# Two-layer diffusion block: all modulation vectors in the first layer, and later places for the block sums of a seven-product feed-forward

## The chip, the cores and the metric

The kernel runs on one core of one Trainium2 chip. The metric is the device time of one execution in microseconds (us); the time of a kernel is the median of its runs. The traces below are each of one profiled execution.

## The reference, cut to what matters

Two layers (`DEPTH = 2`) work on 256 image tokens `x` and 256 context tokens `ctx`, each of width 1024. A layer is a feed-forward, a token mixer (neighbourhood attention beside a pooling branch) and a second feed-forward, each between two norms and each modulated:

```
for l in range(DEPTH):
    mx = mod_vectors(c, w_mod[l], b_mod[l])          # silu(c) @ w_mod + b_mod, split in 9 vectors of 1024
    mc = mod_vectors(c_ctx, w_mod[l], b_mod[l])
    x   = x   + 0.5 * mx[2] * rms(swiglu(rms(x)   * (1 + mx[1]) + mx[0]))     # first feed-forward
    ctx = ctx + 0.5 * mc[2] * rms(swiglu(rms(ctx) * (1 + mc[1]) + mc[0]))
    x, ctx = token mixer with vectors 3, 4, 5
    x, ctx = second feed-forward with vectors 6, 7, 8 (ctx only where l is not the last)
```

A modulation vector depends on `c` and `c_ctx` and on nothing that the layers compute, so it may be computed at any time before it is used. In the last layer the context needs no vector from the sixth (number 5) on. The feed-forward has 2816 hidden columns, 22 blocks of 128. All matmuls are float32 made from two float32r parts, "hi" and "lo" (three matmuls for each product).

## The kernel before, in words

**Stages.** The program runs `ffn(0, 0)`, `token_mix(0)`, `ffn(0, 1)`, `ffn(1, 0)`, `token_mix(1)`, `ffn(1, 1)`. In the trace `ffn(0, 1)` takes from about 605 to 980 us, and `ffn(1, 0)` from about 980 to 1345 us.

**A feed-forward** works through groups of the 22 column blocks. For each block PE multiplies the input `h_big` with the gate and up weights (`pg_ps`, `pu_ps`); ACT and DVE make silu(gate) * up (`tt_wk`) and split it in hi and lo (`g_big`). After a group the down matmuls (`pd_ps`) go over its blocks. Every weight comes by a DMA on SP's queue into one of two `raw` buffers, is rounded to its hi part by ACT, and DVE subtracts to get the lo part (`w_big<-raw_raw,w_big`). All DMAs are issued by SP, in order.

**The seven-product feed-forward.** `ffn(1, 0)` alone (`SEVEN`) multiplies the gate and up weights with seven products of half blocks in the place of eight. After `LEAD = 3` ordinary blocks, each block needs four sums of weight parts on POOL (`prep_seven`: `s12`, `s34`, in the trace `s_wk<-raw_raw` and its like), two more splits on ACT and DVE, and a chain of additions on DVE of what the products leave in PSUM (`c_wk`, `u_wk`) ahead of `tt_wk` and `g_big`. The input needs sums too: `add_up` makes them on POOL in place (`yg_wk<-yg_wk`), and ACT and DVE split them (`ht_big`). The groups (`S_GROUPS`) are of 4, 4, 4, 4 and 6 blocks.

**The modulation.** The vectors 0 and 1 of layer 0 are computed by matmuls at the start. The other 16 lie in the list `todo`, nine steps each. Each of the first eight steps (`mod_steps`) loads 512 KB of `w_mod` (`wm_wk`) and accumulates it on DVE (`acc_wk<-wm_wk,csil`), once for each of the two token streams, or once only for the vectors 5 to 8 of the last layer. The ninth moves each accumulator to another layout with eight 64 KB DMAs (`part_wk<-acc_wk`), folds it with three additions on POOL, sums over partitions with a small matmul (`pm_ps<-sel,part_wk`) and finishes on DVE (`col`); for the vectors 2, 5 and 8 a transposition (`pr_ps`) and one more DMA follow. `fill(rate)`, called after each block of a feed-forward, takes `rate` further steps from the list; `RATE` is 2.6 in the first three feed-forwards.

**The order.** Nothing is issued when it is written. The functions record operations (`Recorder.record`), and `Recorder.order` makes one list out of them: it goes through the operations with prices of its own, and takes next, on the engine that is free first, the one that can start earliest, and among such the one recorded first. An operation's `margin` puts off the time at which this planner thinks it ready. Buffers are places that the planner gives out as well. So the order on each engine is fixed when the program is built, and each engine runs its own list in order, whatever the real times are: an instruction that waits holds up all that stand behind it on its engine.

Of the kernel before, what the change touches and what calls it, by code (L numbers as in the profile page):

```python
# [35 lines left out]
LEAD = 3  # L36
# [3 lines left out]
LIMITS = {"ps": 1}  # L40
RATE = 2.6
BEHIND = 0
MARGIN = 6.0
# [356 lines left out]
def tile_dit_block(  # L400
# [56 lines left out]
    class Stream:  # L457
        def __init__(self):
            self.plan = []
            self.ready = []  # L460
            self.raws = []
            self.taken = 0
            self.ahead = AHEAD

        def add(self, src, parts, seven=False):
# [284 lines left out]
    class Input:  # L750
# [21 lines left out]
        def add_up(self):  # L772
# [3 lines left out]
            for o in range(2):  # L776
                one, two = self.full[ORDER[o]], self.full[ORDER[2 + o]]
                a, b, c, d = one[:, lower, :], two[:, lower, :], two[:, upper, :], one[:, upper, :]
                nc.gpsimd.tensor_sub(a, b, a)
                nc.gpsimd.tensor_sub(b, c, b)  # L780
                nc.gpsimd.tensor_sub(c, c, a)
                nc.gpsimd.tensor_sub(d, d, c)
                for i, src in enumerate((a, c, b, d)):
                    dst = self.sums[i][:, :, :, o * P : (o + 1) * P]
                    split(dst[:, 0], dst[:, 1], src)
# [136 lines left out]
    def ffn(l, ff, both, nxt, rate, lead, parts):  # L922
# [27 lines left out]
        def gate_up(fs, parts):  # L950
# [3 lines left out]
            for part in parts:  # L954
                for f, wg, wup, pg, pu in held:
                    if seven:
# [5 lines left out]
                    if part is parts[-1]:  # L962
                        gate_up_evac(f, pg, pu)
                if seven and part is parts[0]:
                    H["now"].add_up()

# [45 lines left out]
        for gi, (f0, f1) in enumerate(groups):  # L1012
# [4 lines left out]
            elif gi == 0:  # L1017
                gate_up(tuple(range(lead)), parts)
                f = lead
                fill(lead * rate)  # L1020
            while f < f1:
# [4 lines left out]
                f += 1  # L1026
                fill(rate)
            if gi + 1 < len(groups):
# [346 lines left out]
    token_mix(0, (0, 6))  # L1375
    ffn(0, 1, True, (1, 0), RATE, LEAD, (CS, XS))
    ffn(1, 0, True, (1, 3), RATE, LEAD, (0, 1))
    token_mix(1, (1, 6))
    ffn(1, 1, False, None, 0.0, 0, None)

# [105 lines left out]
```

## Time and profile before

| | |
|---|---|
| median of 3 runs | 1677.81 us (1677.76 to 1678.05) |
| the profiled execution | 1681.01 us, its span from the first to the last instruction 1679.1 us |
| mean granted TensorE clock | 0.990 |
| PE busy | 1624.4 us (97%), 9074 matmuls |
| DVE busy | 1276.3 us (76%) |
| ACT, POOL busy | 729.0 us (43%), 363.7 us (22%) |
| DMA | 269.11 MB, mean 160 GB/s |

Idle time of an engine that does not bound the time costs nothing. The page's busy time for PE counts matmuls as pipelined, with ends that are modelled; a gap in it is a time in which PE had nothing it could run. In the timeline a row is: start in us, length in us, engine, line, operation, out<-in, count, and in brackets the engine's idle time before it with what ended it. In a table of stages ("windows") the columns are the stretch, its length, then for each engine its busy time and the count of its instructions, the granted TensorE clock, the DMA engines' share and GB/s. In a list of groups, the busy time and the mean ns of one stand behind the first bar, the idle time before and its releasers behind the second.

### The profile page before, as it was taken

The numbers are of one execution on the slowest core, as the hardware profiler recorded it, in microseconds if no ns is written. First come the engines' busy times: TensorE is split into PE (matmuls) and PEld (weight loads), VectorE is DVE, ScalarE is ACT, GpSimd is POOL, SyncE is SP. The second block draws the span as 40 slices with busy tenths as digits, with TensorE's granted clock in tenths as the row PEclk, the third lists the DMA queues.
The fourth block names the chain that finished last, engine by engine and source line by source line (L and its number), as shares of the span: only waits on it lengthen the run. The fifth ranks groups of instructions, "written<-read, shape, count | busy, mean of one in ns | idle before, by whom it ended". The sixth has DMA issues, their size and how long they took to land.

```text
span 1679.1 us, 23648 instructions
## 1 busy us (share of the span) xinstructions
PE 1624.4 (97%) x9074; PEld 1396.6 (83%) x9074; DVE 1276.3 (76%) x1748; ACT 729.0 (43%) x1287; POOL 363.7 (22%) x348
## 2 busy tenths in 40 slices
PE   6999999999999999999999988999999999899998
PEld 4988888888877798888888888979889888779997
DVE  7987876556789689967745499899989788975664
ACT  7422322225566562232222273433434567664442
POOL 1011111102133211120110064362754022210000
PEclk9999999999999999999999999999999999999999
DMA  9467656631222425765554216354323412355551
GB/s 377 165 233 245 226 176 217 200 104 66 89 73 86 158 101 206 249 212 202 197 187 164 100 42 230 132 187 168 121 101 105 163 57 100 123 199 191 201 197 57
DMA packets 98960, 269.11 MB, mean 160 GB/s; under 512 B 9424, under 2 KB 39328, under 8 KB 87072
## 3 DMA queue, kind: packets, MB, share of 16 engines
q1 hardware_dynamic: 98848, 267.60, 45.7%
q8 instruction: 72, 1.18, 0.3%
q14 instruction: 40, 0.33, 0.1%
HBM read 251.80 MB, written 1.09 MB: 151 GB/s over the span
## 4 chain that ended last, share of the span: by engine, by line
PE 74%; DVE 12%; ACT 5%; issue 3%; DMA 2%; POOL 2%; SPq 1%; POOLq 0%; DVEq 0%; ACTq 0%
PE pd_ps L382 22%; PE pg_ps L382 19%; PE pu_ps L382 19%; PE p_ps L382 6%; DVE w_big L382 3%; PE pk_ps L382 2%; PE pv_ps L382 2%; ACT n_wk L382 2%; POOL rs_st L382 2%; PE pq_ps L382 1%; DVE acc_wk L382 1%; DMA w_big<-in_wmod_dram 1%; ACT sx_wk L382 1%; DVE tt_wk L382 1%; PE pt_ps L382 1%
## 5 line engine op out<-in xcount | busy, mean ns | idle before, releaser
L382 DVE TENSOR_TENSOR w_big<-raw_raw,w_big 128x1024 fp32r<-128x1024 f32 x293 | 374.5, 1291 | 103.2 <-ACT w_big L382 102.5
L382 PE MATMUL pd_ps<-w_big,g_big 128*128 128x512 f32 x1848 | 437.6, 397 | 9.9 <-ACT g_big L382 7.0
L382 PEld LDWEIGHTS pd_ps<-w_big,g_big 128*128 128x128 f32 x1848 | 347.9, 189 | 91.5 <-ACT g_big L382 7.9
L382 ACT ACTIVATE w_big<-raw_raw 128x1024 fp32r<-128x1024 f32 x293 | 302.6, 1053 | 230.9 <-DMA raw_raw<-in_wgu_dram 92.2
L382 PE MATMUL pu_ps<-h_big,w_big 128*128 128x512 f32 (+1 forms) x1944 | 367.8, 342 | 0.0
L382 PEld LDWEIGHTS pu_ps<-h_big,w_big 128*128 128x128 f32 x1944 | 305.6, 189 | 42.6
L382 PE MATMUL pg_ps<-h_big,w_big 128*128 128x512 f32 (+1 forms) x1752 | 331.0, 343 | 2.6 <-ACT h_big L382 1.7
L382 PEld LDWEIGHTS pg_ps<-h_big,w_big 128*128 128x128 f32 x1752 | 276.0, 189 | 43.6 <-ACT h_big L382 2.6
L382 DVE SCALAR_TENSOR_TENSOR acc_wk<-wm_wk,csil,acc_wk 128x1024 f32<-128x1024 f32 x196 | 249.5, 1307 | 41.4 <-DMA wm_wk<-in_wmod_dram 41.3
L382 POOL TENSOR_TENSOR part_wk<-part_wk 128x512 f32<-128x512 f32 (+2 forms) x84 | 89.5, 1066 | 474.6 <-DMA part_wk<-acc_wk 380.8
L382 ACT ACTIVATE g_big<-tt_wk 128x512 fp32r<-128x512 f32 (+1 forms) x84 | 49.2, 585 | 285.5 <-DVE tt_wk L382 283.5
L382 POOL TENSOR_SCALAR rs_st<-sq_st 128x1 f32<-128x1 f32 x24 | 8.3, 346 | 521.0 <-ACT n_wk L382 520.9
L382 POOL TENSOR_TENSOR s_wk<-raw_raw 128x512 f32<-128x512 f32 x38 | 67.4, 1784 | 92.3 <-DMA raw_raw<-in_wgu_dram 39.9
L382 PE MATMUL p_ps<-h_big,w_big 128*128 128x256 f32 x684 | 86.7, 280 | 0.0
L382 PE MATMUL p_ps<-ht_big,w_big 128*128 128x256 f32 x684 | 84.1, 281 | 0.0
L382 PEld LDWEIGHTS p_ps<-h_big,w_big 128*128 128x128 f32 x684 | 83.5, 189 | 0.3
L382 PEld LDWEIGHTS p_ps<-ht_big,w_big 128*128 128x128 f32 x684 | 82.2, 189 | 0.0
L382 ACT ACTIVATE tt_wk<-pg_ps 128x512 f32<-128x512 f32 (+1 forms) x67 | 35.9, 536 | 96.2 <-PE pg_ps L382 73.9
L382 DVE TENSOR_TENSOR g_big<-tt_wk,g_big 128x512 fp32r<-128x512 f32 (+1 forms) x84 | 59.4, 707 | 21.3 <-ACT g_big L382 21.1
L382 DVE TENSOR_TENSOR y_big<-y_big,pd_ps 128x512 f32<-128x512 f32 x72 | 47.1, 680 | 36.0 <-PE pd_ps L382 36.0
L382 PE MATMUL pd_ps<-w_big,mix_big 128*128 128x512 f32 x288 | 72.0, 399 | 0.5 <-DVE mix_big L382 0.5
L382 DVE SCALAR_TENSOR_TENSOR tt_wk<-tt_wk,pg_ps 128x512 f32<-128x512 f32 (+1 forms) x67 | 41.0, 612 | 34.1 <-ACT tt_wk L382 33.6
(159 smaller groups left out, 1851.0 us busy)
## 6 DMA issues: line engine op xcount, KB each, us to landing
raw_raw<-in_wgu_dram SPq DMA_DIRECT2D x84, 1024.0 KB, 4.9
wm_wk<-in_wmod_dram SPq DMA_DIRECT2D x128, 512.0 KB, 6.2
raw_raw<-in_wdn_dram SPq DMA_DIRECT2D x44, 1024.0 KB, 5.1
part_wk<-acc_wk SPq DMA_DIRECT2D x224, 64.0 KB, 2.5
raw_raw<-in_wkq_dram SPq DMA_DIRECT2D x8, 1024.0 KB, 4.7
raw_raw<-in_wout_dram SPq DMA_DIRECT2D x8, 1024.0 KB, 4.9
w_big<-in_wmod_dram SPq DMA_DIRECT2D x7, 1024.0 KB, 12.6
gb_wk<-grow SPq DMA_DIRECT2D x10, 512.0 KB, 6.0
```

Of the source, the lines that this page charges most:

```text
L382: getattr(getattr(nc, op.engine), op.method)(*[self.real(a) for a in op.args], **{k: self.real(a) for k, a in op.kw.items()})
```

## The change

Three things are changed. First, `rate` becomes one number for each group of a feed-forward: 2.6 throughout in `ffn(0, 0)` as before, then 2.6, 4.2 and 5.6 in the three groups of `ffn(0, 1)`, and 0 in `ffn(1, 0)`. With 8, 8 and 6 blocks that is 57 steps and then 88, where 144 are to be done; before it was 57, 57 and the remaining 30. Second, `add_up` is recorded in the middle of the second half of the input in place of the end of the first half, with a margin for the first of its subtractions. Third, the first weight sum of the first seven-product block gets a margin of 12 us in the planner's time.

```diff
-RATE = 2.6
+RATE = (2.6, 2.6, 2.6)
+LATER = (2.6, 4.2, 5.6)
+NONE = (0.0,) * 5
...
+            rec.margin = 0.0 if self.sevens else 2 * MARGIN
+            self.sevens += 1
             nc.gpsimd.tensor_add(s12[:, 0, :], a21, a22)
+            rec.margin = 0.0
...
+                rec.margin = MARGIN
                 a, b, c, d = one[:, lower, :], two[:, lower, :], two[:, upper, :], one[:, upper, :]
                 nc.gpsimd.tensor_sub(a, b, a)
+                rec.margin = 0.0
...
-                for f, wg, wup, pg, pu in held:
+                for i, (f, wg, wup, pg, pu) in enumerate(held):
+                    if seven and part is parts[1] and i == 1:
+                        H["now"].add_up()
...
-                if seven and part is parts[0]:
-                    H["now"].add_up()
...
-                fill(lead * rate)
+                fill(lead * rate[gi])
...
-                fill(rate)
+                fill(rate[gi])
...
-    ffn(0, 1, True, (1, 0), RATE, LEAD, (CS, XS))
-    ffn(1, 0, True, (1, 3), RATE, LEAD, (0, 1))
+    ffn(0, 1, True, (1, 0), LATER, LEAD, (CS, XS))
+    ffn(1, 0, True, (1, 3), NONE, LEAD, (0, 1))
     token_mix(1, (1, 6))
-    ffn(1, 1, False, None, 0.0, 0, None)
+    ffn(1, 1, False, None, NONE, 0, None)
```

Where the instructions move, at three places. PE's own list keeps its order but for the small matmuls of the modulation (`pm_ps`, `pr_ps`).

DVE, the end of the first seven-product block (the fourth of its group) in `ffn(1, 0)`. `c_wk` and `u_wk` gather the products, `tt_wk` is silu(gate) * up, `g_big` its lo part; `w_big` and `wb_wk` are splits of weights of later blocks. Before:

```order
985 L382 TENSOR_TENSOR u_wk_8344<-p_ps_8367,c_wk_8383 128x512
986 L382 TENSOR_TENSOR col_100<-col_100,colt 128x8
987 L382 TENSOR_TENSOR w_big_8300<-raw_raw_8097,w_big_8300 128x1024
988 L382 TENSOR_TENSOR c_wk_8383<-p_ps_8367,u_wk_8344 128x256
989 L382 TENSOR_TENSOR w_big_8319<-raw_raw_8097,w_big_8319 128x1024
990 L382 TENSOR_TENSOR c_wk_8383<-p_ps_8400,u_wk_8344 128x512
991 L382 TENSOR_TENSOR w_big_8430<-raw_raw_8371,w_big_8430 128x1024
992 L382 SCALAR_TENSOR_TENSOR tt_wk_8455<-tt_wk_8455,c_wk_8383 128x512
993 L382 TENSOR_TENSOR wb_wk_8441<-raw_raw_8371,wb_wk_8441 128x512
994 L382 TENSOR_TENSOR tt_wk_8455<-tt_wk_8455,c_wk_8383 128x512
995 L382 TENSOR_TENSOR g_big_8336<-tt_wk_8455,g_big_8336 128x512
```

And the changed kernel at the same place:

```order
1010 L384 TENSOR_TENSOR wb_wk_8487<-raw_raw_8423,wb_wk_8487 128x512
1011 L384 TENSOR_TENSOR u_wk_8461<-p_ps_8491,c_wk_8494 128x512
1012 L384 TENSOR_TENSOR c_wk_8494<-p_ps_8491,u_wk_8461 128x256
1013 L384 TENSOR_TENSOR wb_wk_8529<-raw_raw_8469,wb_wk_8529 128x512
1014 L384 TENSOR_TENSOR w_big_8541<-raw_raw_8423,w_big_8541 128x1024
1015 L384 TENSOR_TENSOR c_wk_8494<-p_ps_8522,u_wk_8461 128x512
1016 L384 SCALAR_TENSOR_TENSOR tt_wk_8572<-tt_wk_8572,c_wk_8494 128x512
1017 L384 TENSOR_TENSOR tt_wk_8572<-tt_wk_8572,c_wk_8494 128x512
1018 L384 TENSOR_TENSOR g_big_8453<-tt_wk_8572,g_big_8453 128x512
```

Nine accumulations (`acc_wk`) that stood between the head of this feed-forward and this point (rows 961 to 983) are gone, two splits from `raw_raw_8097` that stood between `u_wk` and `c_wk` come earlier (rows 1005 and 1007, `raw_raw_8238`), and no split stands between the last `c_wk` and `g_big`.

POOL, the head of `ffn(1, 0)`: the norms of its input (`rs_st`) and the four weight sums of the first seven-product block (`s_wk`). Before:

```order
165 L382 TENSOR_TENSOR rs_st_7758<-rs_st_7758,nhalf 128x1
166 L382 TENSOR_TENSOR s_wk_7798<-raw_raw_7631 128x512
167 L382 TENSOR_TENSOR s_wk_7798<-s_wk_7798,raw_raw_7631 128x512
168 L382 TENSOR_TENSOR s_wk_7803<-raw_raw_7631 128x512
169 L382 TENSOR_SCALAR rs_st_7812<-sq_st_7767 128x1
170 L382 TENSOR_TENSOR rs_st_7812<-rs_st_7812,nhalf 128x1
171 L382 TENSOR_TENSOR s_wk_7803<-raw_raw_7631,s_wk_7798 128x512
```

And the changed kernel:

```order
177 L384 TENSOR_TENSOR rs_st_7910<-rs_st_7910,nhalf 128x1
178 L384 TENSOR_TENSOR s_wk_7946<-raw_raw_7789 128x512
179 L384 TENSOR_SCALAR rs_st_7957<-sq_st_7919 128x1
180 L384 TENSOR_TENSOR rs_st_7957<-rs_st_7957,nhalf 128x1
181 L384 TENSOR_TENSOR s_wk_7946<-s_wk_7946,raw_raw_7789 128x512
182 L384 TENSOR_TENSOR s_wk_7983<-raw_raw_7789 128x512
183 L384 TENSOR_TENSOR s_wk_7983<-raw_raw_7789,s_wk_7946 128x512
```

The first sum stays where it was, and the next two now stand behind one more norm. The sums of the input (`yg_wk<-yg_wk`) stood behind the last of the eight norms before and stand there now.

DVE, the down matmuls of the second group of `ffn(0, 1)` (`y_big` adds what they leave). Before, three accumulations in this stretch:

```order
844 L382 TENSOR_TENSOR w_big_6907<-raw_raw_6814,w_big_6907 128x1024
845 L382 TENSOR_TENSOR w_big_6947<-raw_raw_6814,w_big_6947 128x1024
846 L382 TENSOR_TENSOR w_big_6987<-raw_raw_6899,w_big_6987 128x1024
847 L382 TENSOR_TENSOR y_big_6074<-y_big_6074,pd_ps_6865 128x512
848 L382 TENSOR_SCALAR acc_wk_7011<-wm_wk_6974,csil 128x1024
849 L382 TENSOR_TENSOR y_big_6074<-y_big_6074,pd_ps_6872 128x512
```

And the changed kernel, with twenty in it:

```order
856 L384 TENSOR_SCALAR acc_wk_6995<-wm_wk_6932,csil 128x1024
857 L384 SCALAR_TENSOR_TENSOR acc_wk_6995<-wm_wk_6953,csil,acc_wk_6995 128x1024
858 L384 TENSOR_TENSOR w_big_7010<-raw_raw_6879,w_big_7010 128x1024
859 L384 SCALAR_TENSOR_TENSOR acc_wk_6995<-wm_wk_6964,csil,acc_wk_6995 128x1024
860 L384 SCALAR_TENSOR_TENSOR acc_wk_6995<-wm_wk_6973,csil,acc_wk_6995 128x1024
861 L384 TENSOR_TENSOR w_big_7043<-raw_raw_6956,w_big_7043 128x1024
862 L384 SCALAR_TENSOR_TENSOR acc_wk_6995<-wm_wk_6987,csil,acc_wk_6995 128x1024
863 L384 TENSOR_TENSOR y_big_6076<-y_big_6076,pd_ps_6923 128x512
```

Each accumulation waits for its own DMA (`wm_wk`), and the splits and additions behind it wait with it.

More of the change, by code (lines that the diff above doesn't have):

```diff
@@ L463, in __init__ @@
             self.ahead = AHEAD
+            self.sevens = 0
         def add(self, src, parts, seven=False):
```

## The prediction

> **What bounds the kernel now.** I read the page first, then a table by stage, then the groups and the timeline where that table shows a loss.
>
> ```profile
> PE 1624.4 (97%) x9074; PEld 1396.6 (83%) x9074; DVE 1276.3 (76%) x1748; ACT 729.0 (43%) x1287; POOL 363.7 (22%) x348
> 743.00:944.00 201.00, 201.00 (x884) 164.25 (x883) 123.07 (x133) 53.61 (x67) 17.38 (x18) 1.00 0.51 176
> 833.00:876.00 43.00, 43.00 (x189) 35.34 (x189) 24.02 (x26) 11.60 (x12) 4.99 (x6) 1.00 0.51 172
> 1000.00:1062.00 62.00, 57.24 (x375) 51.62 (x373) 54.99 (x52) 24.62 (x39) 34.41 (x22) 0.94 0.53 181
> 1062.00:1122.00 60.00, 56.34 (x401) 52.44 (x400) 56.89 (x59) 22.37 (x31) 26.44 (x17) 0.97 0.51 182
> 1122.00:1194.00 72.00, 70.38 (x471) 64.06 (x470) 67.51 (x71) 27.25 (x36) 37.57 (x22) 1.00 0.41 140
> 1194.00:1256.00 62.00, 61.78 (x433) 57.33 (x432) 54.41 (x60) 24.67 (x32) 32.72 (x18) 1.00 0.31 107
> ```
>
> PE sets the time: it is busy for 97% of the span. No change of order takes matmuls away here, so only PE's gaps and its low clock can be won. The first two stage rows are the second and third group of ffn(0, 1): PE without a gap, DVE idle for 201.00 - 123.07 = 77.9 us. The other four are the first four groups of the seven-product ffn(1, 0). There PE has gaps in three groups and DVE, not PE, is the full engine: 94% in the second and third. In the fourth group the gaps are gone. What differs between them is the accumulation of modulation vectors, here those instructions alone and then PE's down matmuls of groups one to three and of groups four and five:
>
> ```profile
> 996.00:1200.00 204.00, 37.81 (x26) 0.97 0.47 165
> 1194.00:1345.00 151.00, 0.00 (x0) 1.00 0.36 123
> L382 PE MATMUL pd_ps<-w_big,g_big 128*128 128x512 f32 x288 | 73.1, 413 | 9.7 <-ACT g_big L382 7.0 <-DVE g_big L382 2.7
> L382 PE MATMUL pd_ps<-w_big,g_big 128*128 128x512 f32 x220 | 51.9, 394 | 0.2 <-DVE g_big L382 0.2
> ```
>
> Twenty-six accumulations lie in the first three groups and none in the last two, and 9.7 us of PE's waits lie in the first three against 0.2. All are waits of a down matmul for g_big, the end of the fourth block's chain on DVE. This is a comparison that the kernel makes itself: same code, same PE order, with and without modulation beside it.
>
> The first and largest gap in order of time, with its chain:
>
> ```profile
> 1029.64 13.38 SPq L382 DMA_DIRECT2D raw_raw<-in_wgu_dram  x3
> 1031.29 1.27 DVE L382 SCALAR_TENSOR_TENSOR acc_wk<-wm_wk,csil,acc_wk 128x1024 f32<-128x1024 f32 x1
> 1031.56 5.28 PE L382 MATMUL pd_ps<-w_big,g_big 128*128 128x512 f32 x22
> 1034.43 1.06 ACT L382 ACTIVATE w_big<-raw_raw 128x1024 fp32r<-128x1024 f32 x1 [6.86 <-DMA raw_raw<-in_wgu_dram]
> 1034.70 2.25 DVE L382 TENSOR_TENSOR w_big<-raw_raw,w_big 128x1024 fp32r<-128x1024 f32 x1
> 1037.47 1.72 DVE L382 TENSOR_TENSOR w_big<-raw_raw,w_big 128x1024 fp32r<-128x1024 f32 x1
> 1039.11 1.77 DVE L382 SCALAR_TENSOR_TENSOR tt_wk<-tt_wk,c_wk 128x512 f32<-128x512 f32 x1
> 1040.81 1.75 DVE L382 TENSOR_TENSOR wb_wk<-raw_raw,wb_wk 128x512 fp32r<-128x512 f32 x1
> 1042.47 1.75 DVE L382 TENSOR_TENSOR tt_wk<-tt_wk,c_wk 128x512 f32<-128x512 f32 x1
> 1044.93 16.64 PE L382 MATMUL pd_ps<-w_big,g_big 128*128 128x512 f32 x60 [4.76 <-ACT g_big L382]
> ```
>
> DVE is late, so the two weight buffers come free late, so the next weights are issued only at 1029.64 and ACT waits 6.86 us for them; their splits then stand in DVE's list ahead of tt_wk, and PE waits 4.76 us. After such a gap the clock is low too: 0.94 and 0.97 in the two rows of stages above.
>
> **The change part by part.** *Modulation out of ffn(1, 0).* The pd group of groups four and five gives the pace without disturbance: 51.9 / 220 = 0.2359 us per matmul. Groups one to three have 9.7 us of waits, and 73.1 - 288 x 0.2359 = 5.2 us more in the matmuls, which is the low clock behind the gaps. Together 14.9 us. What remains if the first three groups become like the last two is 0.2 x 288 / 220 = 0.3 us, so -14.6 us. Does the rearranged list allow it at the worst place? Nine accumulations of 1.27 us lay ahead of the row at 1031.29, some 11 us; without them the buffers come free about that much earlier, the splits at 1034.70 and 1037.47 move ahead, and the last stretch of DVE's list is c_wk, two tt_wk and g_big. Even at the slow 1.77 and 1.75 us for tt_wk, from the end of PE's last product (1031.56, where pd_ps begins) two tt_wk, a c_wk and the split in hi and lo need some 5 us, and PE asks for that g_big at 1044.93 - 4.76 = 1040.17. The spare time is about 3 us, so I take the whole gap as gone.
>
> The clock part, at the two gaps of the second group:
>
> ```profile
> 1112.00 0.73 PE L382 MATMUL pd_ps<-w_big,g_big 128*128 128x512 f32 x2 [2.23 <-ACT g_big L382]
> 1114.15 7.42 PE L382 MATMUL pd_ps<-w_big,g_big 128*128 128x512 f32 x24 [1.42 <-DVE g_big L382]
> 1100.00:1120.00 20.00, 16.34 (x69) 12.76 (x68) 20.00 (x19) 5.38 (x7) 17.29 (x11) 0.91 0.61 218
> ```
>
> Neither gap is over 2.3 us, yet the clock fell to 0.91 of that stretch, and the 24 matmuls took 7.42 us for 24 x 0.2359 = 5.7. [...]
>
> *The same work into ffn(0, 1).* Four vectors finish there that finished in ffn(1, 0): 26 accumulations, 32 copies of 64 KB and 12 additions on POOL. What it meets there:
>
> ```profile
> L382 DVE SCALAR_TENSOR_TENSOR acc_wk<-wm_wk,csil,acc_wk 128x1024 f32<-128x1024 f32 x35 | 43.8, 1282 | 6.4 <-DMA wm_wk<-in_wmod_dram 6.3
> L382 ACT ACTIVATE w_big<-raw_raw 128x1024 fp32r<-128x1024 f32 x37 | 38.6, 1053 | 46.6 <-PE pd_ps L382 21.7 <-DMA raw_raw<-in_wgu_dram 12.2 <-PE pu_ps L382 4.9
> 675.99 3.50 POOL L382 TENSOR_TENSOR part_wk<-part_wk 128x512 f32<-128x512 f32 x3 [29.57 <-DMA part_wk<-acc_wk]
> 681.86 0.28 PE L382 MATMUL pm_ps<-sel,part_wk 128*128 128x8 f32 x2
> ```
>
> At 1.282 us, 26 accumulations are 33 us in the 77.9 us that DVE idles in groups two and three. The dense place is the down phase of group two: 17 more there are 24.02 + 17 x 1.282 = 45.8 us in 43 us, 2.8 us too much. It is covered: ACT's splits of weights wait for PE to free their places (21.7 + 4.9 us of the row), so the weights are ahead of PE, and a down phase needs no new g_big. The bytes are 26 x 0.5 MB, in 201 us some 68 GB/s on top of 176. What stands on PE's own list is the small pm_ps matmul: it waits for POOL's fold, that for the copies, those for DVE. In the densest stretch so far the fold was through at 679.49 and PE came at 681.86, 2.4 us later, without a gap. If the vectors of the dense phase come the 2.8 us later, one pm_ps makes PE wait 0.4 us; bounds are 0 and, if the DMA waits of an accumulation (6.4 / 35 = 0.18 us) grow to 0.5 us for all 26, some 8 us. I take +0.8 us, near the low end, as PE has no gap in any feed-forward block with this density.
>
> *The head.* The places that matter for the norms and the sums:
>
> ```profile
> 972.45 0.69 DVE L382 TENSOR_TENSOR h_big<-yg_wk,h_big 128x512 fp32r<-128x512 f32 x1
> 973.53 1.27 POOL L382 TENSOR_TENSOR s_wk<-raw_raw 128x512 f32<-128x512 f32 x1
> 974.88 1.34 POOL L382 TENSOR_TENSOR s_wk<-s_wk,raw_raw 128x512 f32<-128x512 f32 x1
> 975.00 1.76 DVE L382 TENSOR_TENSOR h_big<-yg_wk,h_big 128x512 fp32r<-128x512 f32 x1
> 976.17 1.75 POOL L382 TENSOR_TENSOR s_wk<-raw_raw 128x512 f32<-128x512 f32 x1
> 978.72 0.56 POOL L382 TENSOR_TENSOR rs_st<-rs_st,nhalf 128x1 f32<-128x1 f32 x1
> 979.25 1.30 POOL L382 TENSOR_TENSOR s_wk<-raw_raw,s_wk 128x512 f32<-128x512 f32 x1
> 983.82 0.30 POOL L382 TENSOR_SCALAR rs_st<-sx_st 128x1 f32<-128x1 f32 x1 [3.27 <-ACT n_wk L382]
> ```
>
> The first sum (973.53) keeps its place. The sums at 974.88 and 976.17 now come behind the norm at 978.72: the three then need 1.34 + 1.75 + 1.30 = 4.4 us from 979.28, until 983.7, just ahead of the next norm's start at 983.82. DVE's split beside a running sum took 1.76 us, without one 0.69. So the split at 975.00 gains 1.1 us, and one or two splits between 979 and 984 lose as much each: bounds -1.1 and +2.1, value +0.5. The input's sums stand on POOL behind the same last norm as before, so that part of the change costs and brings nothing; on DVE and ACT only two tt_wk move ahead of splits that PE needs 10 us later.
>
> **The sum**: -14.6 + 0.8 + 0.5 = -13.3 us. It is made from the profiled execution (span 1679.1, 1681.01 us in all); the median of the runs is 1677.81, and I take the same saving from it: **1664.5 us**.
>
> **The rivals.** *Some of the gaps stay* (half the gain). DVE's slow tt_wk, 1.77 us, is slow because POOL's weight sums run beside it, and these stay. Then only what the accumulations themselves take in the three tails goes, about 1.3 + 2 x 1.28 = 3.9 us with 1.7 us of clock: 1677.8 - 5.6 + 1.3 = 1673.5. Against it: the fourth group has POOL at 32.72 of 62 us, as full as the others, and lost 0.2.
>
> *POOL's sums hold up the norms at the head.* Price: if each of the three sums blocks one DVE step of the norm chain for its whole length, +4.4 us in place of +0.5: 1668.4. For it: 1.76 against 0.69 us above. [...]
>
> *The load only moves: ffn(0, 1) becomes DVE's, slower than before.* The place is the stretch from 743 to 944: accumulations wait in DVE's list for DMAs, and g_big and the folds behind them come late. It decides when each of the 26 costs DVE more than 77.9 / 26 = 3.0 us in place of 1.28 + 0.18; at 4 us each it is 104 - 77.9 = 26 us on PE, and 1677.8 - 14.6 + 26 = 1689. Against it: PE has no gap there today at DMA share 0.51.
>
> *The change does nothing for PE*: the gaps are the seven-product block's own and fall elsewhere with DVE at 90%. 1677 to 1679. Against it: groups four and five.
>
> **How the numbers follow.** Forecast (gaps gone, saving 11 to 17 us) 0.63; some gaps stay 0.18; head blocked 0.07; load only moves 0.06; nothing 0.06. The predicted time is the forecast's. Its own range is 1661 to 1667; with the bounds of the head (-1.6, +3.9) and the partial case the range for 8 in 10 is 1659.5 to 1674, which takes in about half of the partial case. About 0.2%, 3.4 us, is what a measurement can tell from no change. Faster by more: 0.63 + 0.18 + 0.07 = 0.88; within: 0.06; slower: 0.06.
>
> **What would show it.** Right: in the three groups between 1000 and 1194 PE's pd_ps row has under 1 us of waits for g_big and a pace near 0.236, the clock is 1.00 in them, and DVE's share falls below 0.85. ffn(0, 1) shows PE without gaps and DVE near 156 of 201 us. Wrong: waits for g_big of over 3 us in ffn(1, 0) say that the sums on POOL, not the modulation, made the gaps; waits of pm_ps for part_wk between 743 and 970 say that the load came too dense; waits of pt_ps or pg_ps over 6 us in all between 970 and 1000 say that the head was blocked.

## The result and the profile after

The changed kernel takes 1667.57 us (median of 4 runs, 1664.02 to 1667.88) against 1677.93 us of the kernel before beside it (1677.76 to 1681.25): a ratio of 0.9929, with a 95% interval of 0.9911 to 0.9947. Forecast were 1664.5 us, with a range of 1659.5 to 1674. A second measurement of the same kernel (the last experiment below) gave 0.9930, 0.9916 to 0.9943. The sign, the place and the reason of the gain came as forecast; three terms were mis-sized.

The stages, in the columns of the tables of stages before: the second and third group of ffn(0, 1), then the first three groups of ffn(1, 0) together and one by one.

```profile
743.00:944.00 201.00, 199.17 (x879) 162.52 (x879) 148.92 (x161) 51.37 (x65) 31.70 (x30) 1.00 0.71 253
833.00:876.00 43.00, 43.00 (x191) 35.43 (x190) 33.43 (x33) 10.80 (x11) 5.42 (x5) 1.00 0.98 343
996.00:1200.00 204.00, 201.25 (x1410) 187.45 (x1411) 161.77 (x175) 86.77 (x118) 94.04 (x55) 0.99 0.29 100
1000.00:1062.00 62.00, 59.74 (x400) 54.33 (x399) 43.88 (x44) 28.77 (x43) 28.71 (x18) 0.97 0.24 85
1062.00:1122.00 60.00, 60.00 (x419) 55.87 (x418) 50.06 (x56) 23.42 (x31) 26.06 (x16) 1.00 0.31 106
1122.00:1194.00 72.00, 72.00 (x518) 67.74 (x518) 59.42 (x67) 29.55 (x39) 35.61 (x20) 1.00 0.29 103
```

DVE's third column fell to 50.06 / 60 = 0.83 and 59.42 / 72 = 0.83 in groups two and three, PE has no gap left there, and the clock is 1.00. In the first group a part of the gap stayed. The down matmuls of the three groups, in the list of groups:

```profile
L384 PE MATMUL pd_ps<-w_big,g_big 128*128 128x512 f32 x288 | 69.4, 402 | 2.3 <-ACT g_big L384 1.5 <-DVE g_big L384 0.7
```

Waits of 9.7 us became 2.3, and 73.1 us of matmuls 69.4. The price is in the first two rows of stages: DVE does 148.92 us in place of 123.07 in ffn(0, 1), PE shows 199.17 of 201 us in place of all, and between 833 and 876 us the DMA engines are at a share of 0.98 in place of 0.51.

The two profiled executions differ by 13.1 us (spans 1679.1 and 1666.0), more than the medians. Some 3 us of that lie ahead of anything that the change touches. Before and then after, two early stretches:

```profile
40.00:80.00 40.00, 40.00 (x265) 37.08 (x265) 37.57 (x52) 21.74 (x40) 1.27 (x2) 0.96 0.46 174
520.00:560.00 40.00, 34.12 (x172) 27.75 (x171) 37.70 (x73) 27.30 (x65) 20.95 (x17) 0.91 0.38 130
```

```profile
40.00:80.00 40.00, 40.00 (x270) 36.73 (x269) 37.81 (x51) 20.91 (x39) 1.26 (x2) 1.00 0.47 175
520.00:560.00 40.00, 34.14 (x181) 27.92 (x180) 37.26 (x74) 27.57 (x65) 21.09 (x17) 0.96 0.45 154
```

The same work meets a granted clock of 0.96 and 0.91 in the one, 1.00 and 0.96 in the other: 0.04 x 40 + 0.05 x 40 = 3.6 us. So it is in part chance that the two spans differ by nearly the forecast 13.3 us. To compare executions stage by stage I add up, over PE's matmuls in a trace, how much later each starts than a fixed pace after the one ahead of it (0.2295 us for 512 columns, 0.1165 for 256, 0.11 for a transposition; the medians of these steps in the trace before are 0.231, 0.118 and 0.109): gaps and low clock together (a start that comes a little sooner than the pace counts negative). This loss, in us:

| execution | to 600 | 600 to 960, ffn(0, 1) | 960 to 1000, head | 1000 to 1060, group 1 | 1060 to 1200, groups 2, 3 | rest | sum |
|---|---|---|---|---|---|---|---|
| before | 31.2 | 2.8 | 7.6 | 7.7 | 9.4 | 20.0 | 78.7 |
| changed | 28.1 | 4.7 | 7.1 | 4.9 | 1.8 | 19.0 | 65.5 |
| changed, second profile | 30.6 | 5.6 | 7.5 | 1.7 | 1.8 | 18.9 | 66.1 |
| e1 rates only | 30.1 | 4.8 | 6.5 | 2.6 | 1.6 | 19.1 | 64.7 |
| e2 places only | 30.9 | 2.7 | 5.7 | 9.3 | 9.5 | 19.4 | 77.5 |
| e3 no accumulations | 28.7 | 2.7 | 7.6 | 1.0 | 3.1 | 19.1 | 62.2 |
| e4 no weight sums | 30.2 | 2.7 | 3.9 | 2.4 | 1.5 | 19.6 | 60.3 |
| e5 split later | 28.1 | 5.9 | 7.6 | 0.4 | 1.7 | 19.2 | 62.9 |
| e6 end of a vector later | 28.9 | 8.2 | 7.8 | 1.9 | 2.2 | 19.8 | 68.8 |
| e7 no margin at the head | 29.7 | 3.8 | 7.1 | 0.4 | 1.8 | 19.0 | 61.8 |
| e8 more in ffn(0, 0) | 39.0 | 5.0 | 4.7 | 3.2 | 1.8 | 19.3 | 73.0 |
| e9 fewer DMAs | 30.0 | 2.5 | 7.6 | 1.5 | 1.5 | 19.0 | 62.1 |
| e10 even rates | 30.3 | 16.6 | 4.8 | 2.8 | 1.6 | 20.3 | 76.4 |
| e11 rates between | 28.0 | 4.1 | 6.5 | 1.2 | 1.0 | 19.8 | 60.6 |

The rows are single executions; what is ahead of 600 us varies from 28.0 to 31.2 us where nothing was changed there (e8 apart), so the verdicts below rest on the medians and intervals, and the table tells where.

### The profile page after: what moved, and what is told of

It reads as the page before. It is cut to its first block, busy times and chain, and to the rows that moved or that the text cites. A ratio compares the mean times of both kernels' runs of the same rounds, so it can differ in the third digit from the quotient of the medians.

```text
span 1666.0 us, 23609 instructions
## 1 busy us (share of the span) xinstructions
PE 1616.9 (97%) x9074; PEld 1392.0 (84%) x9074; DVE 1265.1 (76%) x1748; ACT 730.0 (44%) x1287; POOL 359.7 (22%) x348
## 4 chain that ended last, share of the span: by engine, by line
PE 67%; DVE 14%; DMA 5%; ACT 4%; issue 4%; SPq 3%; POOL 2%; DVEq 0%; POOLq 0%; ACTq 0%
PE pd_ps L384 21%; PE pu_ps L384 14%; PE pg_ps L384 13%; PE p_ps L384 11%; DVE acc_wk L384 4%; DMA wm_wk<-in_wmod_dram 3%; SPq L384 3%; DVE w_big L384 3%; PE pk_ps L384 2%; PE pv_ps L384 2%; ACT n_wk L384 2%; POOL rs_st L384 2%; PE pq_ps L384 1%; DVE tt_wk L384 1%; DMA w_big<-in_wmod_dram 1%
## 5 line engine op out<-in xcount | busy, mean ns | idle before, releaser
L384 DVE TENSOR_TENSOR w_big<-raw_raw,w_big 128x1024 fp32r<-128x1024 f32 x293 | 370.4, 1277 | 117.8 <-ACT w_big L384 109.4
L384 POOL TENSOR_TENSOR part_wk<-part_wk 128x512 f32<-128x512 f32 (+2 forms) x84 | 92.9, 1107 | 492.6 <-DMA part_wk<-acc_wk 414.5
L384 DVE TENSOR_TENSOR w_big<-s_wk,w_big 128x1024 fp32r<-128x1024 f32 x38 | 58.2, 1531 | 15.0 <-ACT w_big L384 15.0
```

The source lines that it names most:

```text
L384: getattr(getattr(nc, op.engine), op.method)(*[self.real(a) for a in op.args], **{k: self.real(a) for k, a in op.kw.items()})
```

## The experiments

**Which part of the change does it.** The first run keeps only the rates, the second only the places.

```diff
 # e1, against the changed kernel
-            rec.margin = 0.0 if self.sevens else 2 * MARGIN
-            self.sevens += 1
...
-                rec.margin = MARGIN
                 a, b, c, d = one[:, lower, :], two[:, lower, :], two[:, upper, :], one[:, upper, :]
...
-                    if seven and part is parts[1] and i == 1:
-                        H["now"].add_up()
...
+                if seven and part is parts[0]:
+                    H["now"].add_up()
 # e2, against the changed kernel
-LATER = (2.6, 4.2, 5.6)
+LATER = (2.6, 2.6, 2.6)
...
-    ffn(1, 0, True, (1, 3), NONE, LEAD, (0, 1))
+    ffn(1, 0, True, (1, 3), (2.6,) * 5, LEAD, (0, 1))
```

> The changed kernel with its new rates alone: the sums of the input are recorded at the end of the first half as before, and neither they nor the first weight sum have a margin. My theory (the 26 accumulations leaving ffn(1, 0) are the whole gain, the head costs about half a microsecond to one): 1666 to 1668 us, pd_ps waits for g_big about 2 us as in the changed kernel, and the wait of pg_ps near 983 us back from 2.43 us to about 0.9. Rival (the later sums are what empties the gaps): 1674 us or more, with over 5 us of pd_ps waits.

> The changed kernel with the rates of the kernel before (2.6 everywhere, so the last 30 steps run in ffn(1, 0) again): only the later record of the input's sums and the two margins remain. My theory: nothing that can be measured, 1676.5 to 1679.5 us, pd_ps waits in ffn(1, 0) near 10 us, PE's gaps at the head about 1 us more. Rival (the later sums are what empties the gaps): 1670 us or less, pd_ps waits under 5 us.

Measured: e1 1667.1 us, ratio 0.9928 (0.9915 to 0.9940), the same as the whole change; e2 1678.97 us, ratio 1.0003 (0.9994 to 1.0012), no change. The down matmuls of the first three groups, e1 and then e2:

```profile
L384 PE MATMUL pd_ps<-w_big,g_big 128*128 128x512 f32 x288 | 67.7, 394 | 1.7 <-ACT g_big L384 1.0 <-DVE g_big L384 0.7
```

```profile
L384 PE MATMUL pd_ps<-w_big,g_big 128*128 128x512 f32 x288 | 74.8, 420 | 7.1 <-DVE g_big L384 4.9 <-ACT g_big L384 2.2
```

The rates are the whole gain, as far as the runs can tell. The later input sums and the margins bring nothing that can be measured.

**Is it DVE's time or the DMAs, and what share have POOL's sums?** Two kernels made from the one before: one leaves accumulations out and keeps their DMAs, the other keeps every accumulation and takes POOL's weight sums away.

```diff
 # e3, against the kernel before
                 for v in streams:
+                    if l == DEPTH - 1 and (j > 5 and k > 0 or j == 5 and k > 5):
+                        continue
 # e4, against the kernel before
-            nc.gpsimd.tensor_add(s12[:, 0, :], a21, a22)
-            nc.gpsimd.tensor_sub(s12[:, 1, :], s12[:, 0, :], a11)
-            nc.gpsimd.tensor_sub(s34[:, 0, :], a11, a21)
-            nc.gpsimd.tensor_sub(s34[:, 1, :], a12, s12[:, 1, :])
+            nc.gpsimd.memset(s12, 0.0)
+            nc.gpsimd.memset(s34, 0.0)
```

> The kernel before, with 23 of the 26 accumulations in ffn(1, 0) left out (the last two of vector 5 of the last layer, and of its vectors 6, 7 and 8 all but the first each); their DMAs, folds and small matmuls stay, so those vectors hold only part of their sums. Nothing is added to ffn(0, 1). My theory (DVE's time for the accumulations makes the gaps): 1663 to 1666 us, pd_ps waits of the first three groups under 2 us, DVE in 996 to 1200 us at about 160. Rival (the 13 MB of modulation weights delay the feed-forward's weights, and DVE waits with them): 1674 us or more, waits of DVE and ACT for raw_raw as long as before, pd_ps waits over 6 us.

> The kernel before, with POOL's four weight sums of each seven-product block replaced by two memsets, so the products made with those sums are wrong; every accumulation stays in ffn(1, 0). Theory that DVE is simply too full (accumulations of 1.28 us and operations that POOL's sums stretch from 0.68 to about 1.7 us add up, and relief of either kind is enough): DVE's time between 996 and 1200 us falls from 189 us to under 172, pd_ps waits under 3 us, 1664 to 1668 us. Rival (the gaps come from where the accumulations stand in DVE's list and from the two weight buffers that come free late, so POOL's sums matter little): pd_ps waits 6 us or more, 1673 to 1678 us.

Measured: e3 1664.88 us, ratio 0.9919 (0.9906 to 0.9933); e4 1662.84 us, ratio 0.9907 (0.9893 to 0.9920), below the 1664 to 1668 us of its theory. The stretch of three groups before; then the same stretch with its down matmuls in e3, and in e4:

```profile
996.00:1200.00 204.00, 193.96 (x1315) 178.12 (x1314) 189.39 (x193) 79.96 (x112) 105.77 (x63) 0.97 0.47 165
```

```profile
996.00:1200.00 204.00, 202.59 (x1437) 188.69 (x1436) 172.27 (x183) 86.07 (x119) 102.78 (x65) 1.00 0.49 172
L382 PE MATMUL pd_ps<-w_big,g_big 128*128 128x512 f32 x288 | 68.5, 396 | 1.4 <-DVE g_big L382 1.4
```

```profile
996.00:1200.00 204.00, 202.77 (x1441) 189.17 (x1440) 170.91 (x208) 86.90 (x121) 46.39 (x43) 1.00 0.50 173
L382 PE MATMUL pd_ps<-w_big,g_big 128*128 128x512 f32 x288 | 68.3, 396 | 1.0 <-ACT g_big L382 1.0
```

The DMA share is 0.49 and 0.50, as before the change (0.47), and the gaps are gone in both: the DMAs of the modulation did not make them. In both DVE falls from 189.39 to about 171 of 204 us, by two different reliefs. (e3 kept more DVE time than the 160 expected, since PE got further in the same stretch, 1437 matmuls in place of 1315, and brought more work with it.) So the first theory's cause is not the accumulations alone: DVE was too full by the sum of the accumulations and of what POOL's sums add to its operations. Two things blur this. The planner made a new order for each kernel, so neither is a pure subtraction; and e4 also brings the sums to ACT sooner (ACT waited 9.7 us for them in this stretch before, 2.2 us in e4), which no run separates from the relief of DVE. The sums coming late cannot make the gaps alone, since e3 keeps the sums and lost them. What they add, on the accumulations and the split of `wb_wk` in that stretch, before and then e4:

```profile
L382 DVE SCALAR_TENSOR_TENSOR acc_wk<-wm_wk,csil,acc_wk 128x1024 f32<-128x1024 f32 x23 | 33.5, 1457 | 2.9 <-DMA wm_wk<-in_wmod_dram 2.8
L382 DVE TENSOR_TENSOR wb_wk<-raw_raw,wb_wk 128x512 fp32r<-128x512 f32 x12 | 17.3, 1445 | 0.1
L382 DVE TENSOR_TENSOR c_wk<-p_ps,u_wk 128x512 f32<-128x512 f32 x18 | 12.3, 682 | 1.1 <-PE p_ps L382 1.1
```

```profile
L382 DVE SCALAR_TENSOR_TENSOR acc_wk<-wm_wk,csil,acc_wk 128x1024 f32<-128x1024 f32 x23 | 29.7, 1293 | 5.6 <-DMA wm_wk<-in_wmod_dram 5.6
L382 DVE TENSOR_TENSOR wb_wk<-raw_raw,wb_wk 128x512 fp32r<-128x512 f32 x13 | 10.5, 810 | 0.5 <-ACT wb_wk L382 0.5
L382 DVE TENSOR_TENSOR c_wk<-p_ps,u_wk 128x512 f32<-128x512 f32 x23 | 15.8, 687 | 4.6 <-PE p_ps L382 4.5
```

A split of `wb_wk` takes 1445 ns on average in the kernel with the sums and 810 in the one with memsets, an accumulation 1457 and 1293; `c_wk`, which reads one operand from PSUM, takes 682 and 687. These are means over a stretch in which POOL was busy for 105.77 of 204 us before and for 46.39 in e4. Why some operations are stretched and `c_wk` is not, no run shows.

**The gap that stayed in the first group.** On DVE in the changed kernel, with PE's two waits, in order of time:

```profile
1032.16 1.23 DVE L384 TENSOR_TENSOR wb_wk<-raw_raw,wb_wk 128x512 fp32r<-128x512 f32 x1 [2.67 <-ACT wb_wk L384]
1033.32 2.32 DVE L384 TENSOR_TENSOR w_big<-raw_raw,w_big 128x1024 fp32r<-128x1024 f32 x1
1035.56 0.68 DVE L384 TENSOR_TENSOR c_wk<-p_ps,u_wk 128x512 f32<-128x512 f32 x1
1038.65 1.68 DVE L384 TENSOR_TENSOR tt_wk<-tt_wk,c_wk 128x512 f32<-128x512 f32 x1
1041.04 0.74 PE L384 MATMUL pd_ps<-w_big,g_big 128*128 128x512 f32 x2 [1.51 <-ACT g_big L384]
1042.53 7.66 PE L384 MATMUL pd_ps<-w_big,g_big 128*128 128x512 f32 x25 [0.75 <-DVE g_big L384]
```

PE's products were done at about 1031, but `c_wk` stands in DVE's list behind the split of a weight buffer for a block two ahead. ACT could begin that split only at 1031.50 (5.62 us of waiting for the DMA), and DVE sat idle for 2.67 us, for the last 1.0 of them with `c_wk`'s input there (PE's last product ended at 1031.16). The edit puts that split off in the planner:

```diff
+            rec.margin = MARGIN if self.sevens in (2, 3) else 0.0
             split(wb[:, 0, :], wb[:, 1, :], a22)
+            rec.margin = 0.0
```

> The changed kernel with a margin of 6 us in the planner's time on the hi/lo split of one half-size weight (wb_wk) of the second and third seven-product block, so that on DVE c_wk, tt_wk and g_big of the first seven-product block stand ahead of the split from the weight buffer that landed only at 1031.5 us. My theory (the gaps of 1.51 and 0.75 us that stay in the first group come from that late buffer, whose split stands ahead of c_wk): pd_ps waits under 0.5 us, loss between 1020 and 1060 us from 4.9 to about 1 us, 1663 to 1665 us. Rival (tt_wk of 1.6 us beside POOL's sums is the cause, and the gap stays): pd_ps waits 1.5 us or more, 1667 to 1668 us.

Measured: 1665.97 us (1663.55 to 1667.26), ratio 0.9924 (0.9911 to 0.9936), and DVE and the down matmuls:

```profile
1030.97 2.30 DVE L384 TENSOR_TENSOR w_big<-raw_raw,w_big 128x1024 fp32r<-128x1024 f32 x1
1033.19 0.68 DVE L384 TENSOR_TENSOR c_wk<-p_ps,u_wk 128x512 f32<-128x512 f32 x1
L384 PE MATMUL pd_ps<-w_big,g_big 128*128 128x512 f32 x288 | 67.2, 394 | 0.0
```

The gap is gone and the loss of the stretch fell from 4.9 to 0.4 us in the trace, though `tt_wk` still takes 1.60 and 1.67 us. With that split no longer ahead of `c_wk` the gap is gone in this execution; a gain in the time is not shown (1665.97 us lies above the 1663 to 1665 of the theory, and 1.3 to 1.6 us against the changed kernel lie within the intervals). Run e7 and the last run below show why.

**The head.** Without the first margin:

```diff
-            rec.margin = 0.0 if self.sevens else 2 * MARGIN
+            rec.margin = 0.0
```

> The changed kernel without the 12 us of margin of the first weight sum; the later sums of the input stay. My theory (the margin puts three of POOL's weight sums beside the split of h_big that PE waits for, 3.45 us for two in place of 1.28): the wait of pg_ps near 980 us falls from 2.43 to about 0.9 us, and the whole gains 0.5 to 1 us: 1666.5 to 1667.2 us. Rival (the sums stretch another operation of the head for as long, wherever they stand): the loss between 970 and 1000 us stays at about 7 us, and the time at 1667.6.

Measured: 1665.68 us, ratio 0.9925 (0.9912 to 0.9937). The changed kernel at the place that the prediction priced:

```profile
975.16 0.68 DVE L384 TENSOR_TENSOR h_big<-yg_wk,h_big 128x512 fp32r<-128x512 f32 x1
979.46 1.74 POOL L384 TENSOR_TENSOR s_wk<-raw_raw 128x512 f32<-128x512 f32 x1
979.97 3.45 DVE L384 TENSOR_TENSOR h_big<-yg_wk,h_big 128x512 fp32r<-128x512 f32 x2
983.47 2.74 PE L384 MATMUL pg_ps<-h_big,w_big 128*128 128x256 f32 x21 [2.43 <-DVE h_big L384]
```

And in e7, PE's waits between 970 and 1000 us:

```profile
L384 PE MATMUL pg_ps<-h_big,w_big 128*128 128x256 f32 x51 | 6.7, 280 | 0.0
L384 PE MATMUL pt_ps<-ident,n_wk 128*128 128x128 f32 x24 | 4.4, 331 | 4.3 <-DVE n_wk L384 3.5 <-ACT n_wk L384 0.8
```

The wait of `pg_ps` is gone; the transpositions wait 4.3 us in place of 3.2. The loss of the head is 7.1 us in both, as the rival said, but not for its reason. PE's waits there add up to 4.3 us in e7 against 5.6 and 4.8 in the two profiles of the changed kernel (and 4.3 before the change), so the margin costs some 0.5 to 1.4 us of waits. What hides this is the clock: it is at one half from 977.41 to 980.82 us in e7, and nowhere in the head of the first profile of the changed kernel (granted clock 0.94 and 1.00 between 970 and 1000 us). The median is 1.6 to 1.9 us under that of the changed kernel, below what either theory said and within the intervals. The first group's gap is gone too, with DVE's list there in the same order, because the late buffer landed earlier: ACT's splits of the two buffers stand at 1026.71 and 1030.25, 3.5 us apart, in place of 6.3.

**The price in ffn(0, 1).** PE's waits there, and those of the accumulations, in the changed kernel between 743 and 944 us:

```profile
L384 DVE SCALAR_TENSOR_TENSOR acc_wk<-wm_wk,csil,acc_wk 128x1024 f32<-128x1024 f32 x56 | 71.9, 1306 | 22.4 <-DMA wm_wk<-in_wmod_dram 22.0
L384 PE MATMUL pm_ps<-sel,part_wk 128*128 128x8 f32 x24 | 3.5, 218 | 0.7 <-POOL part_wk L384 0.7
L384 PE MATMUL pr_ps<-ident,col 128*16 128x128 f32 (+1 forms) x2 | 0.5, 272 | 1.1 <-DVE col L384 1.1
```

The accumulations waited 22.4 us for their DMAs in place of 6.4. Three runs ask whether this can be had cheaper: a later place for the end of a vector (e6), another distribution (e8), and the DMAs alone (e9). Two more distributions follow below.

```diff
 # e6, against the changed kernel, in last() and in finish_mod()
-                rec.margin = MARGIN
+                rec.margin = 2 * MARGIN
 # e8
-RATE = (2.6, 2.6, 2.6)
-LATER = (2.6, 4.2, 5.6)
+RATE = (2.6, 2.6, 5.6)
+LATER = (2.6, 3.4, 4.0)
 # e9
+        held = []
...
-                wm = wtile([P, D], "wm")
-                nc.sync.dma_start(out=wm, in_=wmod[l, j, k])
+                if l == DEPTH - 1 and j >= 2 and k > 0:
+                    wm = held[0]
+                else:
+                    wm = wtile([P, D], "wm")
+                    nc.sync.dma_start(out=wm, in_=wmod[l, j, k])
+                    held.append(wm)
```

> The changed kernel with 12 us in place of 6 us of margin for the small matmul (pm_ps) and the transposition (pr_ps) that end a vector, everywhere. My theory (in ffn(0, 1) the only cost of the denser load is PE standing at pm_ps, 0.87 us, and at pr_ps, 1.29 us, because the accumulations ahead of them wait for DMAs): both waits gone, 1664.5 to 1666 us. Rival (the whole chain is late by more than 6 us, or the later matmul holds its place in PSUM and makes others wait): a wait of over 0.5 us for part_wk, col or a PSUM place stays between 743 and 944 us, 1667 us or more.

> The changed kernel with other rates: 5.6 in the third group of ffn(0, 0), then 2.6, 3.4 and 4.0 in ffn(0, 1), so that the down matmuls between 833 and 876 us have fewer accumulations beside them. My theory (ffn(0, 1) lost some 2.4 us to waits for late vectors where the DMA share was 0.98): the waits of pm_ps and pr_ps in ffn(0, 1) are gone, the DMA share in that stretch falls to about 0.8, nothing is lost in ffn(0, 0): 1664.5 to 1666 us. Rival (ffn(0, 0) has no room either, its small matmuls wait there): 1667 us or more with new PE gaps before 390 us.

> The changed kernel with most DMAs of modulation weights in ffn(0, 1) left out: each vector of the last layer from the third on (number 2) loads only its first 512 KB and accumulates that eight times, so these vectors are wrong; all accumulations on DVE, folds and small matmuls stay. My theory (in ffn(0, 1) the DMAs at a share of 0.98 between 833 and 876 us make the accumulations late, and with them the pm_ps and pr_ps that PE waits for): DVE's waits for wm_wk between 743 and 944 us fall from 22.4 us to under 5, the waits of 0.87 and 1.29 us on PE are gone, 1664 to 1666 us. Rival (DVE itself is too dense there): the same PE waits stay although the DMA share is under 0.5.

Measured: e9 1664.23 us, ratio 0.9915 (0.9902 to 0.9929). Its accumulations, and the stretch from 833 to 876 us:

```profile
L384 DVE SCALAR_TENSOR_TENSOR acc_wk<-wm_wk,csil,acc_wk 128x1024 f32<-128x1024 f32 x56 | 77.1, 1391 | 0.8
833.00:876.00 43.00, 43.00 (x191) 35.46 (x190) 41.24 (x38) 9.05 (x10) 13.61 (x9) 1.00 0.51 153
```

DVE is fuller there than in the changed kernel (41.24 of 43 us), yet the waits of `pm_ps` and `pr_ps` are gone and ffn(0, 1) loses 2.5 us, less than before the change. So it is the DMAs that cost there, not DVE. At a share of 0.98 they moved 343 GB/s in the changed kernel. That rate was not the most they could move, since ten of those 43 us moved 412 GB/s:

```profile
840.00:850.00 10.00, 10.00 (x46) 8.26 (x45) 9.90 (x12) 2.70 (x4) 0.00 (x0) 1.00 1.03 412
```

So not the rate but the share of the DMA engines' time, 0.98 in the 43 us, is what says here that next to nothing was left (it adds up the times of packets, and is 1.03 in that row).

e6: 1667.69 us (1666.21 to 1671.81), ratio 0.9942 (0.9929 to 0.9956), no better than the change; the rival is right. The profiled execution took 1671.29 us, so its trace shows more loss than the median has. The waits of the small matmuls went, and a larger one came, of a down matmul for the place in PSUM that a later-finished vector still held (DVE's list, then PE):

```profile
856.42 1.28 DVE L384 SCALAR_TENSOR_TENSOR acc_wk<-wm_wk,csil,acc_wk 128x1024 f32<-128x1024 f32 x1 [1.65 <-DMA wm_wk<-in_wmod_dram]
858.98 3.45 PE L384 MATMUL pd_ps<-w_big,g_big 128*128 128x512 f32 x8 [3.71 <-DVE col L384]
```

e8: 1674.7 us, ratio 0.9978 (0.9968 to 0.9987), most of the gain lost; the rival is right again. The DMA share between 833 and 876 us fell to 0.77 as expected, yet `pr_ps` still waited 1.7 us in ffn(0, 1). In the last group of ffn(0, 0):

```profile
397.10 2.00 ACT L384 ACTIVATE w_big<-raw_raw 128x1024 fp32r<-128x1024 f32 x2 [11.69 <-DMA raw_raw<-in_wv_dram]
400.07 2.07 PE L384 MATMUL pd_ps<-w_big,g_big 128*128 128x512 f32 x4 [6.12 <-DVE y_big L384]
```

The weights of the token mixer came late behind modulation weights, DVE stood 4.66 us at their split, and `y_big`, which frees the PSUM place that PE wants, stood behind it in DVE's list.

**Other rates in ffn(0, 1)**, both without the head's margin: even ones, and some between those and the change's.

```diff
 # e10
-LATER = (2.6, 4.2, 5.6)
+LATER = (3.9, 3.9, 4.3)
 # e11
-LATER = (2.6, 4.2, 5.6)
+LATER = (3.2, 4.0, 5.0)
```

> The changed kernel without the margin of the first weight sum, and with rates of 3.9, 3.9 and 4.3 in ffn(0, 1) in place of 2.6, 4.2 and 5.6. My theory (what the change loses in ffn(0, 1) comes from the densest stretch, and the free time of the first group is not used): no wait over 0.5 us on PE in ffn(0, 1), 1663 to 1665 us. Rival (any group whose rate is near 4 fills the DMA queues in its down phase, since they catch up there what the blocks could not take): waits of PE of 1 to 4 us in the first or second group's down phase, 1666 us or more.

> As the run before, with rates of 3.2, 4.0 and 5.0 in ffn(0, 1). My theory: between the two, 1663.5 to 1666 us, waits of pm_ps and pr_ps in ffn(0, 1) together under 1 us. Rival (the place of a single small matmul decides, not the rate): a wait of 1 us or more stays somewhere in ffn(0, 1), 1665.5 to 1667.5 us.

Measured: e10 1678.29 us, ratio 0.9999 (0.9990 to 1.0008): the whole gain is gone. In its first group (POOL, DVE, PE; the third row is the split of a weight that PE waits for):

```profile
698.76 4.75 POOL L384 TENSOR_TENSOR part_wk<-part_wk 128x512 f32<-128x512 f32 x3 [16.65 <-DMA part_wk<-acc_wk]
699.22 3.97 DVE L384 SCALAR_TENSOR_TENSOR acc_wk<-wm_wk,csil,acc_wk 128x1024 f32<-128x1024 f32 x2
703.12 1.47 DVE L384 TENSOR_TENSOR w_big<-raw_raw,w_big 128x1024 fp32r<-128x1024 f32 x1
704.64 5.91 PE L384 MATMUL pd_ps<-w_big,g_big 128*128 128x512 f32 x18 [4.55 <-DVE w_big L384]
```

Two accumulations took 3.97 us beside a fold on POOL, and the split that the next matmuls need stood behind them. This is the largest of three such waits in ffn(0, 1), 8.2 us in all (1.29, 4.55 and 2.39); with 1.9 us of waits for `part_wk` and two stretches of half clock behind the gaps (granted clock 0.92 between 705 and 743 us) ffn(0, 1) lost 16.6 us. That is the rival "the load only moves" of the prediction, at another place than it named. e11 took 1663.06 us (1661.83 to 1665.38), ratio 0.9911 (0.9898 to 0.9925), the fastest median of those that do the whole work, with a wait of 1.3 us of `pm_ps` left, as its rival said, and a time below both forecasts. Its interval overlaps with that of the change, so a further gain of 3 to 4 us is likely, not shown; against e7, which has the same head, it is 2.6 us.

**The changed kernel once more.**

> The changed kernel as it is, once more, to know its own spread (1664.02 to 1667.88 us in four runs), since the runs on the first group's gap and on the rates differ from it by 2 to 4 us. My theory (the gaps of 1.5 and 0.75 us in the first group are in its fixed order and stay in every execution; the spread comes from where the low clock falls): median 1666.5 to 1668 us, pd_ps waits of 2 to 2.5 us again, loss between 1000 and 1060 us of 4 to 5 us again. Rival (the profile shown was an unlucky execution, and the kernel is as fast as the run with the later split): median 1665.5 to 1666.3 us, pd_ps waits under 1.5 us.

Measured: 1667.25 us (1665.04 to 1668.59), ratio 0.9930 (0.9916 to 0.9943), the time that my theory gave. The trace does not follow it:

```profile
L384 PE MATMUL pd_ps<-w_big,g_big 128*128 128x512 f32 x288 | 67.5, 394 | 0.8 <-DVE g_big L384 0.8
970.00:1000.00 30.00, 25.45 (x156) 22.40 (x154) 26.60 (x40) 22.15 (x52) 16.72 (x18) 0.94 0.10 35
```

The order is the same, and the late buffer's DMA was issued 3.47 us after the one ahead of it in both executions, but it landed 3.9 us after that one (ACT's splits at 1029.17 and 1033.02) in place of 6.3 (1025.25 and 1031.50), so the first group lost 1.7 us in place of 4.9. In its stead `pm_ps` waited 2.0 us in ffn(0, 1), and the clock at the head was 0.94, where the first profile had 1.00:

```profile
970.00:1000.00 30.00, 24.35 (x168) 21.72 (x168) 28.31 (x40) 22.29 (x48) 20.30 (x18) 1.00 0.11 36
```

So the remaining gap is an arrangement that costs something when a DMA comes late, not a fixed 4 us.

## Why the prediction was right, and where its terms were off

**What bounds the kernel** held. PE's gaps in groups one to three were what could be won, and taking the accumulations out of ffn(1, 0) won most of them (e1, e3). Of the signs named beforehand, the clock of 1.00 came in groups two and three and DVE's share below 0.85 in all three; the waits for `g_big` were 2.3 us, between the marks for right (1) and wrong (3), and 0.8 us in the second profile; and `pm_ps` did wait for `part_wk` (0.7 and 2.0 us), the sign of a load that came too dense. The comparison of groups one to three with four and five was the right one to make.

**The main term, -14.6 us.** The size of the prize was right: where the gap of the first group is gone as well, in e5, the loss from 1000 to 1200 us falls from 17.1 to 2.1 us, by 15.0. The change itself won 10.4 us there in the one profile and 13.6 in the other. The step that failed is "so I take the whole gap as gone". It reckoned the chain from PE's last product to `g_big` at some 5 us, with the splits out of the way. That left out ACT's silu and the hand-overs between ACT and DVE: even in e5 it takes 6.4 us from the start of the last `c_wk` (1033.19) to the end of `g_big` (1039.63), which the spare time still covers. In the list as built the split of the second buffer stood ahead of `c_wk`, and its DMA was late; the chain took from 1031 to 1042.5. The rows that showed it were at hand: the order listed `wb_wk_8529` ahead of the last `c_wk`.

**The clock** behaved as the rows of before said. With the gaps gone it is 1.00 in groups two and three, and the saving holds the 5.2 us of low clock: 67.2 us for the 288 matmuls in e5 against 73.1. In the changed kernel gaps of 1.51 and 0.75 us were enough: the clock of the stretch from 1000 to 1062 us was 0.97. Narrower stretches show how: first those two gaps in the changed kernel and what follows them, then two stretches of the head, one in its first profile and one in its second.

```profile
1039.74:1043.15 3.41, 1.36 (x5) 0.83 (x6) 2.71 (x3) 1.66 (x3) 2.55 (x3) 1.00 0.02 7
1043.15:1046.56 3.41, 3.41 (x10) 2.64 (x9) 1.54 (x1) 1.71 (x3) 3.33 (x3) 0.50 0.00 0
981.71:985.12 3.41, 1.66 (x14) 1.66 (x15) 3.41 (x5) 0.96 (x3) 1.34 (x2) 1.00 0.00 0
984.65:988.06 3.41, 1.38 (x11) 1.39 (x12) 3.41 (x5) 1.23 (x3) 1.42 (x1) 1.00 0.00 0
```

Between 60 and 1640 us of every trace here the low clock is one half for 3.41 or 6.83 us, and within a trace these falls begin whole multiples of 3.413 us apart: before at 541.40, 995.38, 1043.16, 1114.84 and 1483.48 us, which is 133, 14, 21 and 108 steps. I laid that grid of windows over the fourteen profiles in the same stretch (PE's busy time with its modelled ends). Of the 40 falls from full to half clock, 39 come right after a window in which PE was busy for at most 1.47 of 3.41 us, and one after 1.69 us; of the 6387 windows at full clock that were followed by full clock none has PE busy for less than 1.56 us. (In the profiles before and after alone: 8 falls, each after at most 1.47 us, and 904 windows at full clock, none below 1.65 us.) So what these traces show ahead of a fall is a window of 3.41 us with PE busy for at most 1.47 us of it, 43%, and once for 1.69. The 1.51 and 0.75 us fell into one such window, with 1.36 us of work. In the head a border of the grid lies at 981.71 us in one execution of the changed kernel and at 984.65 in the other; the window from there holds 1.66 us of work in the one, where the clock stays at 1.00, and 1.38 in the other, where it is one half from 988.06 to 991.47 and the head has 0.94. What sets the place of the grid, no run shows.

**ffn(0, 1), +0.8 us**, was too small: 4.7 and 5.6 us of loss against 2.8, so +1.9 and +2.8. The place (the down phase of group two) and the victim (`pm_ps`) were named rightly, the resource was not. The forecast reckoned DVE's time in the 43 us, and the DMAs only as a mean over 201 us (68 GB/s on top of 176). In the dense 43 us they ran at 343 GB/s, DVE stayed at 33.43 us instead of the 45.8 forecast, and the accumulations came later instead: 15 ran in those 43 us, 9 more than before and not 17. The upper bound of 8 us, from longer DMA waits, was the right mechanism: they grew from 0.18 to 22.4 / 56 = 0.40 us for each accumulation.

**The head, +0.5 us**: the two effects came as described. The split at 975.16 took 0.68 in place of 1.76 us, and two splits behind it took 3.45 us, so that PE waited 2.43 us in place of 0.86. PE's waits in the head rose from 4.3 to 5.6 us (4.8 in the second profile), inside the bounds of -1.1 and +2.1. In the sum of losses the head still stands at 7.1 and 7.5 against 7.6, -0.5 and -0.1: the kernel before lost a stretch of half clock there (995.38 to 998.79), the first profile of the changed kernel none. That the total did not suffer is luck.

**The total.** By stage the two profiles give -10.4 + 1.9 - 0.5 = -9.0 and -13.6 + 2.8 - 0.1 = -10.9 in these three places, and -1.0 in the rest; the medians differ by 10.4 and, in the second measurement, 12.6. The forecast of -13.3 was too good by 0.7 to 2.9 us.

**The rivals.** "Some of the gaps stay" came partly true, in the first group, but not by the cause given: with the split out of the way the slow `tt_wk` cost nothing (e5). Yet the statement against it, that POOL's sums do not matter because the fourth group has them too, was too strong: without them the accumulations cost nothing either (e4). "The sums hold up the norms" did not come about as a loss in the table, and in PE's waits only by 0.5 to 1.3 us. "The load only moves" did not happen with these rates, and did with rates that differ by 1.3 steps per block in the first group (e10); 0.06 was little for a cliff so near.

## What to carry to other kernels

Where an engine is nearly full, ask for all that fills it, the stretching by a neighbour among it (1445 ns in place of 810 for a split of `wb_wk`): two quite different reliefs of 17 and 18.5 us of DVE time took away the same gaps. Work that moves into idle time has to be budgeted for each resource over the densest tens of microseconds where it lands (here 43 us at a DMA share of 0.98, where the mean of 201 us was 0.71), DMAs first, since an in-order list that waits for a DMA holds up everything behind it (here 22.4 us of waits in DVE's list). And when a gap is taken as gone, read in the new order what stands ahead of the late instruction and when its data land.

## What was not expected of the hardware

The landing of the same 1 MB transfer, issued 3.47 us after the one ahead of it each time, came 3.9 or 6.3 us after that one's, and with it a stretch of 60 us lost 1.7 or 4.9 us; why it came late is open. The clock at the head was 1.00 or 0.94 for the same kernel: it fell to one half for 3.41 us in the execution in which a window of the 3.413 us grid held 1.38 us of PE's work, and not in the one in which it held 1.66. And an accumulation of 1.28 us took about 2 us beside a fold on POOL (3.97 us for two), where the mean in ffn(0, 1) had been 1.28 us before.
